# The delta rule's values turned token-major by block transposes and DRAM instead of products of the identity

## The chip, the core and the metric

The kernel runs on one core of a Trainium2 chip. The metric is device time in microseconds. The profile names TensorE's matmuls PE and its weight loads PEld, VectorE DVE, ScalarE ACT, GpSimd POOL; SPq is the queue of SyncE, from which nearly all DMAs are issued.

## The reference, cut to what matters

One encoder layer over 256 tokens of width 2048, in f32. The normalised input h feeds two token mixers, retention and a gated delta rule; their gated sum goes through an output projection; cross-attention, an MLP of width 8192 and a last norm follow. The change is in the delta rule, which has 16 heads of width 128:

```python
gqkv = jax.nn.silu(causal_conv(gqkv, conv_w)).astype(f32)
gq, gk, gv = jnp.split(gqkv, [GDN_HEADS * GDN_DK, 2 * GDN_HEADS * GDN_DK], axis=-1)
...
gv = gv.reshape(b, s, GDN_HEADS, GDN_DV)
...
u = t @ (vc * bc)            # values, token by token, into the chunk's triangular system
...
v_new = u_i - w_i @ state
```

The convolution and the SiLU act on every value channel along the tokens; the triangular system then needs the values with tokens on the rows.

## The kernel before

Weights are streamed once. `fetch` loads 1 MB into `raw` (three buffers, issued on SP), ScalarE rounds each half into `whi` (L108), VectorE takes the rest into `wlo` (L111), and TensorE multiplies both with the input held in SBUF. `blocks` gives 256 output channels as rows with the tokens along them (products L193 and L194); `chunk` gives tokens as rows (L151 to L153).

The delta rule's heads come in four groups of four, each group (`gdn_stream`) in two pairs of heads. For a pair, three calls of `blocks` give q, k and v channels. `evac` sends each head's 128 rows through `conv_silu`: ScalarE scales by the last tap, VectorE adds three shifted taps (L549), ScalarE applies the SiLU (L551). For v the result is the tile `vt`, 128 channels x 256 tokens, one for each head. The squares of q (L587, from the same two-slot tag as the accumulator) and the Gram products of k and q (L594 to L598) follow, then the decay factors (`alt`) and copies of small blocks of them (`cmp_l`, `pair32`, `pair64`). Near the end of the head's work TensorE transposes `vt` in two 128x128 products with the identity into a PSUM bank (L637), and ScalarE copies them to the head's part of `r4`, scaled by `nk`, the norm of k (L640). `r4` (one buffer, four heads) is read much later, by the triangular products of `gdn_core` (L722, L751), whose steps are dealt out between weight loads of the following stages; those of a group are finished before the next group takes `r4`.

Two round trips through DRAM are there already: `gdn_blocks` writes `cmp_l` to `scr_l` and reads it back as `lw`, and writes `tw` to `scr_t` and reads it back as `ct`; VectorE turns `ct` in 32x32 blocks into `cu` (L670).

The order of instructions on each engine, SP among them, is written by a planner that simulates the program in advance. Weight loads, their rounding and the evacuation of results have raised priority in it. At run time each engine and each queue goes through its list in order, and an instruction that waits holds up those behind it.

Of the kernel before, what the change touches and what calls it, by code (L numbers as in the profile page):

```python
# [10 lines left out]
F32 = mybir.dt.float32  # L11
F32R = mybir.dt.float32r
I32 = mybir.dt.int32
AF = mybir.ActivationFunctionType
# [3 lines left out]
P = 128  # L18
D = 2048
S = 256  # L20
NT = S // P
# [3 lines left out]
GH, GD = 16, 128  # L25
# [26 lines left out]
def trunk(ctx: ExitStack, tc: tile.TileContext, x, mem, positions, norm_mix_g, w_in, conv_w, gdn_a_log, gdn_dt_bias,  # L52
          ret_gn_g, gdn_norm_g, w_out, norm_x_g, norm_mem_g, w_xq, w_xkv, w_xo, norm_ffn_g, w_ff1, w_ff2,
          norm_final_g, inv_freq, out):
    nc = tc.nc
    PSUM = bass.MemoryType.PSUM
    act, vec, pool, pe = nc.scalar, nc.vector, nc.gpsimd, nc.tensor
# [7 lines left out]
    dram = ctx.enter_context(tc.tile_pool(name="scr", bufs=2, space=bass.MemoryType.DRAM))  # L65
# [6 lines left out]
    def bank():  # L72
        return psp.tile([P, 512], F32, name="b", tag="b", bufs=4)
# [10 lines left out]
    def finish_steps():  # L84
        while steps:
            step()
# [121 lines left out]
    ident = cp.tile([P, P], F32, name="ident")  # L208
# [129 lines left out]
    for k2 in range(8):  # L338
        ps = bank()
# [24 lines left out]
    for a in range(2):  # L364
        ps = bank()
# [166 lines left out]
    mx = mixer.enter_context(tc.tile_pool(name="mix", bufs=2))  # L532
# [8 lines left out]
    t64, u64, u128 = sparse("t64", 64), sparse("u64", 64), sparse("u128", NT, P)  # L541


    def conv_silu(blk, ps, dst):
        acc = mx.tile([P, S], F32, name="acc", tag="acc", bufs=2)
        act.activation(acc, ps, AF.Copy, scale=cw[:, 3, blk:blk + 1])  # L546
        for j in range(2, -1, -1):
            d = 3 - j
            vec.scalar_tensor_tensor(acc[:, d:], ps[:, :S - d], cw[:, j, blk:blk + 1], acc[:, d:],  # L549
                                     op0=ALU.mult, op1=ALU.add)  # L550
        act.activation(dst, acc, AF.Silu)  # L551

    def diag(alt):
        return alt.rearrange("p a n -> p (a n)")[:, 0:512].rearrange("p (t n) -> p t n", t=NT)[:, :, 0:P]

    def gdn_stream(grp):

        heads = []
        qe4 = mx.tile([P, 4, NT], F32, name="qe4", tag="qe4", bufs=2)
        for pr in range(2):  # L560
            h0 = grp * 4 + pr * 2
            dec = mx.tile([P, 2, 384], F32, name="dec", tag="dec", bufs=1)
            nc.sync.dma_start(dec, dec_d[h0:h0 + 2].rearrange("h p n -> p h n"))
            kq = mx.tile([P, 2, 2, S], F32, name="kq", tag="kq", bufs=1)
            vts = []
            for part, c0, bofs in ((1, C_GQ, 0), (0, C_GK, 16), (2, C_GV, 32)):
                def evac(b, ps, part=part, bofs=bofs):
                    if part < 2:
                        conv_silu(bofs + h0 + b, ps, kq[:, b, part, :])
                    else:  # L570
                        vt = mx.tile([P, S], F32, name="vt", tag="vt", bufs=2)
                        conv_silu(bofs + h0 + b, ps, vt)
                        vts.append(vt)
                blocks(h1, w_in[0], c0 + h0 * GD, 2, evac)
            if pr == 0:
                finish_steps()
                cmp_l = mx.tile([P, 8, 32], F32, name="cmp_l", tag="cmp", bufs=1)
                r4 = mx.tile([P, 4, NT, GD], F32, name="r4", tag="r4", bufs=1)
            grams = []
            ssk = mx.tile([P, 2, NT], F32, name="ssk", tag="ssk", bufs=2)  # L580
            for b in range(2):
                kh = mx.tile([P, 2, S], F32R, name="kh", tag="kh", bufs=2)
                kl = mx.tile([P, 2, S], F32R, name="kl", tag="kl", bufs=2)
                sq = mx.tile([P, S], F32, name="sq", tag="acc", bufs=2)
                act.activation(kh, kq[:, b], AF.Copy)
                vec.tensor_sub(kl, kq[:, b], kh.bitcast(F32))
                act.activation(sq, kq[:, b, 1], AF.Square)  # L587
                g0, g1 = bank(), bank()
                g0v = g0.rearrange("p (a n) -> p a n", a=2)
                g1v = g1[:, 0:256].rearrange("p (a n) -> p a n", a=2)  # L590
                if b == 0:
                    ssq = g1[:, 256:260].rearrange("p (b i) -> p b i", b=2)
                for t in range(NT):
                    pe.matmul(ssq[:, b, t:t + 1], sq[:, t * P:(t + 1) * P], ones[:, :1], start=True, stop=True)  # L594
                for n, (l, r) in enumerate(((kh, kh), (kh, kl), (kl, kh))):
                    pe.matmul(g0v, l[:, 0, 0:P], r, start=n == 0, stop=n == 2)  # L596
                for n, (l, r) in enumerate(((kh, kh), (kh, kl), (kl, kh))):
                    pe.matmul(g1v, l[:, 0, P:S], r[:, :, P:S], start=n == 0, stop=n == 2)  # L598
                grams.append((g0v, g1v))
                for t, src in enumerate((g0v[:, 0, 0:P], g1v[:, 0, :])):  # L600
                    dj = sm.tile([P, S], F32, name="dj", tag="bo", bufs=2)[:, :P]
                    vec.scalar_tensor_tensor(dj, src, 1.0, ident, op0=ALU.mult, op1=ALU.mult,
                                             accum_out=ssk[:, b, t:t + 1])
            ske = mx.tile([P, 2, NT], F32, name="ske", tag="ske", bufs=2)
            vec.tensor_scalar(ske, ssk, EPS, None, op0=ALU.add)
            vec.tensor_scalar(qe4[:, 2 * pr:2 * pr + 2, :], ssq, EPS * GD, EPS * EPS * GD,
                              op0=ALU.mult, op1=ALU.add)
            sc = mx.tile([P, 2, NT], F32, name="sc", tag="sc", bufs=2)
            vec.reciprocal(sc, ske)
            vec.tensor_mul(sc, sc, beta[:, :, h0:h0 + 2].rearrange("p t h -> p h t"))  # L610
            nk = mx.tile([P, 2, NT], F32, name="nk", tag="nk", bufs=2)
            pool.tensor_tensor(nk.rearrange("p b t -> p (b t)"), ske.rearrange("p b t -> p (b t)"), half_pow[:, :4], op=ALU.pow)
            for b in range(2):
                h, slot = h0 + b, pr * 2 + b
                g0v, g1v = grams[b]

                alt = mx.tile([P, 2, 384], F32, name="alt", tag="alt", bufs=4)
                vec.scalar_tensor_tensor(alt[:, :, 0:S], g0v, sc[:, b, 0:1],
                                         dec[:, b, 0:256].unsqueeze(1).to_broadcast([P, 2, 256]),
                                         op0=ALU.mult, op1=ALU.mult)  # L620
                vec.scalar_tensor_tensor(alt[:, :, S:384], g1v, sc[:, b, 1:2],
                                         dec[:, b, 256:384].unsqueeze(1).to_broadcast([P, 2, P]),
                                         op0=ALU.mult, op1=ALU.mult)
                for q in range(4):
                    ps_ = slice(32 * q, 32 * q + 32)
                    act.activation(cmp_l[ps_, 2 * slot:2 * slot + 2, :], diag(alt)[ps_, :, 32 * q:32 * q + 32], AF.Copy)

                for t in range(NT):
                    for a in range(2):
                        to, at = 64 * t + 32 * a, 64 * a  # L630
                        act.activation(pair32[to:to + 32, slot, to:to + 32],
                                       diag(alt)[at:at + 32, t, at + 32:at + 64], AF.Copy)
                    act.activation(pair64[64 * t:64 * t + 64, slot, 64 * t:64 * t + 64], diag(alt)[0:64, t, 64:P], AF.Copy)

                vps = bank()
                for t in range(NT):
                    pe.transpose(vps[:, t * P:(t + 1) * P], vts[b][:, t * P:(t + 1) * P], ident)  # L637
                r = r4[:, slot, :, :]
                for t in range(NT):
                    act.activation(r[:, t, :], vps[:, t * P:(t + 1) * P], AF.Copy, scale=nk[:, b, t:t + 1])  # L640
                heads.append(alt)
        return heads, cmp_l, r4, qe4

# [217 lines left out]
    for j in range(5):  # L861
        if j < 4:
            heads, cmp_l, r4, qe4 = gdn_stream(j)
# [80 lines left out]
    for h in range(XH):  # L944
# [17 lines left out]
        pr = xa.tile([P, NT, S], F32, name="pr", tag="pr", bufs=2)  # L962
# [36 lines left out]
    for c in range(4):  # L999
        for t in range(NT):  # L1000
            ps = bank()
# [95 lines left out]
```

## Time and profile before

| | |
|---|---|
| median of 3 runs | 2084.81 us (2084.80 to 2086.04) |
| the profiled execution, whole / its span | 2084.04 us / 2082.3 us |
| TensorE busy | 2066.1 us, 99% of the span |
| VectorE, ScalarE, GpSimd busy | 1402.3, 1120.3, 30.7 us |
| data moved by DMA | 405.90 MB in 314168 packets, 16288 of them under 512 B |
| granted clock of TensorE | 0.999 over the span |

Busy times are unions of an engine's instructions; matmuls are pipelined, their ends are modelled, and a second one begins before the first one's end. Lines such as L193 are those of the kernel before. In the timeline a row may merge several instructions (x3), and the bracket at its end says how long the engine was idle before it and what it waited for.

### The profile page before, as it was taken

How to read it: one execution, taken by the hardware profiler on the slowest of the kernel's cores; microseconds unless marked ns; L12 is line 12 of the kernel's file. 1: busy time of each engine (PE TensorE's matmuls, PEld its weight loads, DVE VectorE, ACT ScalarE, POOL GpSimd, SP SyncE). 2: the span in 40 equal slices, each digit the busy share in tenths (PEclk: the TensorE clock that was granted, in tenths of full speed). 3: DMA queues.
4: the chain of work that ended last, by engine and by line, in shares of the span. 5: the costliest groups of instructions: out<-in, count | busy, mean ns of one | idle time of the engine just before them, and what ended most of it. 6: DMA issues, size and time to landing. Idle time of an engine off the chain costs nothing.

```text
span 2082.3 us, 28611 instructions
## 1 busy us (share of the span) xinstructions
PE 2066.1 (99%) x11044; PEld 1783.3 (86%) x11044; DVE 1402.3 (67%) x2226; ACT 1120.3 (54%) x1844; POOL 30.7 (1%) x37
## 2 busy tenths in 40 slices
PE   8999999999999999999999999999999999999998
PEld 6888888888888888888888899888888888888887
DVE  5766879778757885778557665766556546645655
ACT  7674664675547555655446564654444434434444
POOL 0000000000000000000000000000000000000000
PEclk9999999999999999999999999999999999999999
DMA  8787666556555655565467664666566556656653
GB/s 299 246 274 248 199 192 195 166 179 194 188 162 190 193 179 164 188 187 189 152 214 239 193 189 146 187 198 193 191 194 191 193 191 192 192 195 189 194 191 141
DMA packets 314168, 405.90 MB, mean 195 GB/s; under 512 B 16288, under 2 KB 222128, under 8 KB 313904
## 3 DMA queue, kind: packets, MB, share of 16 engines
q1 hardware_dynamic: 313744, 403.55, 61.2%
q8 instruction: 86, 1.41, 0.3%
q10 hardware_dynamic: 288, 0.52, 0.1%
q14 instruction: 50, 0.41, 0.1%
HBM read 390.40 MB, written 13.65 MB: 194 GB/s over the span
## 4 chain that ended last, share of the span: by engine, by line
PE 97%; DMA 1%; ACT 1%; SPq 1%; DVE 0%; issue 0%; POOLq 0%; POOL 0%; ACTq 0%; DVEq 0%
PE s L193 33%; PE s L194 17%; PE s L152 14%; PE s L151 14%; PE s L153 14%; PE b L689 1%; PE b L596 1%; DMA xc<-x 1%; PE b L722 1%; PE b L122 0%; PE b L121 0%; PE b L123 0%; SPq L292 0%; ACT dec_w L501 0%; PE b L598 0%
## 5 line engine op out<-in xcount | busy, mean ns | idle before, releaser
L111 DVE TENSOR_TENSOR wlo<-raw,whi 128x1024 fp32r<-128x1024 f32 x702 | 857.8, 1223 | 515.1 <-ACT whi L108 508.5
L108 ACT ACTIVATE whi<-raw 128x1024 fp32r<-128x1024 f32 x702 | 742.7, 1059 | 688.7 <-PE s L153 341.7
L193 PE MATMUL s<-q,whi 128*128 128x512 f32 x3088 | 1062.4, 390 | 0.3 <-DVE q L986 0.3
L194 PE MATMUL s<-q,wlo 128*128 128x256 f32 x3088 | 845.0, 281 | 0.8 <-DVE wlo L111 0.8
L193 PEld LDWEIGHTS s<-q,whi 128*128 128x128 f32 x3088 | 570.7, 188 | 110.5 <-DVE q L986 0.5
L194 PEld LDWEIGHTS s<-q,wlo 128*128 128x128 f32 x3088 | 579.2, 188 | 14.3 <-DVE wlo L111 2.7
L152 PE MATMUL s<-wlo,q 128*128 128x512 f32 x1264 | 495.6, 392 | 0.7 <-DVE wlo L111 0.7
L153 PE MATMUL s<-whi,q 128*128 128x512 f32 x1264 | 492.2, 390 | 0.0
L151 PE MATMUL s<-whi,q 128*128 128x512 f32 x1264 | 451.5, 390 | 1.6 <-ACT q L255 1.6
L151 PEld LDWEIGHTS s<-whi,q 128*128 128x128 f32 x1264 | 237.3, 188 | 50.8 <-ACT q L255 2.0
L152 PEld LDWEIGHTS s<-wlo,q 128*128 128x128 f32 x1264 | 237.7, 188 | 48.9 <-DVE wlo L111 1.5
L153 PEld LDWEIGHTS s<-whi,q 128*128 128x128 f32 x1264 | 237.7, 188 | 47.7
L200 ACT ACTIVATE bo<-s 128x256 f32<-128x256 f32 x193 | 73.1, 379 | 119.2 <-PE s L194 106.0
L201 DVE TENSOR_TENSOR bo<-bo,s 128x256 f32<-128x256 f32 x193 | 80.4, 417 | 44.5 <-ACT bo L200 44.2
L549 DVE SCALAR_TENSOR_TENSOR acc<-bo,cw,acc 128x255 f32<-128x255 f32 (+1 forms) x144 | 66.8, 479 | 3.1 <-ACT acc L546 1.2
L658 DVE TENSOR_TENSOR pr<-lw,tw 32x31 f32<-32x31 f32 (+15 forms) x124 | 40.4, 326 | 10.7 <-DMA lw<-scr_l 8.6
L660 DVE TENSOR_TENSOR tw<-tw,pr 32x31 f32<-32x31 f32 (+15 forms) x124 | 40.6, 327 | 2.0
L1025 DVE SCALAR_TENSOR_TENSOR res<-s,rstd3q,res 128x512 f32<-128x512 f32 (+1 forms) x32 | 22.3, 735 | 12.0 <-PE s L153 12.0
L823 ACT ACTIVATE gth<-s 128x512 f32<-128x512 f32 x32 | 19.0, 592 | 20.7 <-PE s L153 15.1
L1014 DVE SCALAR_TENSOR_TENSOR hs<-bo 128x256 f32<-128x256 f32 x64 | 27.0, 421 | 1.1
L1017 DVE TENSOR_TENSOR q<-hs,q 128x256 fp32r<-128x256 f32 x64 | 26.8, 419 | 0.8 <-ACT q L1016 0.8
L1016 ACT ACTIVATE q<-hs 128x256 fp32r<-128x256 f32 x64 | 26.2, 410 | 0.0
(300 smaller groups left out, 1074.8 us busy)
## 6 DMA issues: line engine op xcount, KB each, us to landing
raw<-w_in SPq DMA_DIRECT2D x144, 1024.0 KB
raw<-w_ff SPq DMA_DIRECT2D x128, 1024.0 KB
raw<-w_xkv SPq DMA_DIRECT2D x31, 1024.0 KB
raw<-w_out SPq DMA_DIRECT2D x16, 1024.0 KB
raw<-w_xq SPq DMA_DIRECT2D x16, 1024.0 KB
raw<-w_xo SPq DMA_DIRECT2D x16, 1024.0 KB
dec_d<-dec_w SPq DMA_DIRECT2D x8, 384.0 KB
dec<-dec_d SPq DMA_DIRECT2D x8, 384.0 KB
```

The source lines that it names most:

```text
L108: rounding = act.activation(hi, src, AF.Copy)
L111: vec.tensor_sub(lo, src, hi.bitcast(F32))
L151: pe.matmul(o, xh, wh, start=first, stop=False)
L152: pe.matmul(o, xh, wl, start=False, stop=False)
L153: pe.matmul(o, xl, wh, start=False, stop=last)
L193: pe.matmul(ps[b], lh, xhl, start=kk == 0, stop=False)
L194: pe.matmul(ps[b][:, :S], ll, xh, start=False, stop=kk == KT - 1)
L200: act.activation(o, ps[b][:, S:], AF.Copy)
L201: vec.tensor_add(o, o, ps[b][:, :S])
L549: vec.scalar_tensor_tensor(acc[:, d:], ps[:, :S - d], cw[:, j, blk:blk + 1], acc[:, d:], op0=ALU.mult, op1=ALU.add)
L658: vec.tensor_mul(pv, lw[:, j, j + 1:32].unsqueeze(2).to_broadcast([32, n, j + 1]), tw[:, j, 0:j + 1].unsqueeze(1).to_broadcast([32, n, j + ...
L660: vec.tensor_sub(tw[:, j + 1:32, 0:j + 1], tw[:, j + 1:32, 0:j + 1], pv)
```

## The change

`conv_silu` gets a flag. With it (for v alone) the SiLU is written in place into the accumulator, and VectorE turns that, 128x256, in 32x32 blocks into the head's half of `vt`, which is now one tile for the pair, with one buffer. After the three `blocks` of a pair, four DMAs (one for each 32 partitions of `vt`) write the blocks to a DRAM tile `v_d` so that each token's 128 values stand in one row, in runs of 32 values (128 bytes); a fifth DMA reads `v_d` back into the pair's part of `r4`, tokens on the partitions. The two transposing products of each head and their PSUM bank go; the scaling by `nk` is done in place on `r4`.

```diff
-    def conv_silu(blk, ps, dst):
+    def conv_silu(blk, ps, dst, blocks_of=False):
...
-        act.activation(dst, acc, AF.Silu)
+        act.activation(acc if blocks_of else dst, acc, AF.Silu)
+        if blocks_of:
+            vec.transpose(dst, acc)
...
-            vts = []
+            vt = mx.tile([P, 2, S], F32, name="vt", tag="vt", bufs=1)
...
-                        vt = mx.tile([P, S], F32, name="vt", tag="vt", bufs=2)
-                        conv_silu(bofs + h0 + b, ps, vt)
-                        vts.append(vt)
+                        conv_silu(bofs + h0 + b, ps, vt[:, b], blocks_of=True)
...
+            v_d = dram.tile([2, S, GD], F32, name="v_d", tag="v_d", bufs=2)
+            for a in range(4):
+                nc.sync.dma_start(v_d[:, :, 32 * a:32 * a + 32].rearrange("h (b i) f -> i (h b) f", i=32),
+                                  vt[32 * a:32 * a + 32].rearrange("i h (b f) -> i (h b) f", f=32))
+            nc.sync.dma_start(r4[:, 2 * pr:2 * pr + 2], v_d.rearrange("h (t p) f -> p h t f", p=P))
...
-                vps = bank()
-                for t in range(NT):
-                    pe.transpose(vps[:, t * P:(t + 1) * P], vts[b][:, t * P:(t + 1) * P], ident)
                 r = r4[:, slot, :, :]
                 for t in range(NT):
-                    act.activation(r[:, t, :], vps[:, t * P:(t + 1) * P], AF.Copy, scale=nk[:, b, t:t + 1])
+                    act.activation(r[:, t, :], r[:, t, :], AF.Copy, scale=nk[:, b, t:t + 1])
```

## Rows read from the trace of the kernel before

**Rows 1.** The page, part 1: busy us, share of the span, instructions.

```profile
PE 2066.1 (99%) x11044; PEld 1783.3 (86%) x11044; DVE 1402.3 (67%) x2226; ACT 1120.3 (54%) x1844; POOL 30.7 (1%) x37
```

**Rows 2.** Busy us by stretch; then granted clock, DMA share, GB/s.

```profile
200.00:1293.00 1093.00, 1093.00 (x5955) 948.33 (x5954) 805.46 (x1424) 621.87 (x1089) 26.25 (x25) 1.00 0.59 186
```

**Rows 3.** Groups by line and form, L637: busy us, mean ns, idle before.

```profile
L637 PE MATMUL b<-ident,vt 128*128 128x128 f32 x32 | 6.1, 271 | 0.0
```

**Rows 4.** Timeline of TensorE's products: start us, us, instruction, count.

```profile
256.53 0.39 PE L193 MATMUL s<-q,whi 128*128 128x512 f32 x1
256.76 0.38 PE L637 MATMUL b<-ident,vt 128*128 128x128 f32 x2
...
257.09 0.39 PE L193 MATMUL s<-q,whi 128*128 128x512 f32 x1
...
257.44 0.38 PE L637 MATMUL b<-ident,vt 128*128 128x128 f32 x2
...
258.01 0.63 PE L193 MATMUL s<-q,whi 128*128 128x512 f32 x2
...
258.72 0.39 PE L193 MATMUL s<-q,whi 128*128 128x512 f32 x1
...
260.09 0.39 PE L193 MATMUL s<-q,whi 128*128 128x512 f32 x1
```

**Rows 5.** Instructions on the tile cu: ns min/median/max, first and last start.

```profile
L670 DVE STREAM_TRANSPOSE cu<-ct x4: 439/446/449, 371.3 to 973.8; 128x256 f32<-128x256 f32 x4
```

**Rows 6.** Groups by line and form on VectorE and ScalarE.

```profile
L111 DVE TENSOR_TENSOR wlo<-raw,whi 128x1024 fp32r<-128x1024 f32 x702 | 857.8, 1223 | 515.1 <-ACT whi L108 508.5
...
L200 ACT ACTIVATE bo<-s 128x256 f32<-128x256 f32 x193 | 73.1, 379 | 119.2 <-PE s L194 106.0 <-DVE dj L602 13.1
...
L640 ACT ACTIVATE r<-b,nk 128x128 f32<-128x128 f32 x32 | 9.6, 366 | 0.1
...
L551 ACT ACTIVATE vt<-acc 128x256 f32<-128x256 f32 x16 | 6.5, 406 | 0.3
```

**Rows 7.** Timeline of ScalarE, from 247 to 262 us.

```profile
247.29 0.40 ACT L551 ACTIVATE vt<-acc 128x256 f32<-128x256 f32 x1
247.72 0.42 ACT L587 ACTIVATE sq<-kq 128x256 f32<-128x256 f32 x1
251.40 0.38 ACT L200 ACTIVATE bo<-s 128x256 f32<-128x256 f32 x1 [3.26 <-DVE dj L602]
...
258.17 0.62 ACT L640 ACTIVATE r<-b,nk 128x128 f32<-128x128 f32 x2
```

**Rows 8.** Instructions on the tile ct: its reads as SP issues them.

```profile
L668 SPq DMA_DIRECT2D ct<-scr_t x16: 313/452/647, 363.8 to 967.5; - x16
```

**Rows 9.** Timeline of the SP queue, from 200 to 310 us.

```profile
216.68 32.35 SPq L98 DMA_DIRECT2D raw<-w_in  x7
256.72 0.37 SPq L563 DMA_DIRECT2D dec<-dec_d  x1
257.85 27.82 SPq L98 DMA_DIRECT2D raw<-w_in  x6
...
297.30 0.34 SPq L647 DMA_DIRECT2D scr_l<-cmp_l  x1
302.23 0.71 SPq L650 DMA_DIRECT2D lw<-scr_l  x2
303.03 0.41 SPq L98 DMA_DIRECT2D raw<-w_in  x1
```

**Rows 10.** Waits of the SP queue: total us, times, longest.

```profile
SPq L668 <- DMA scr_t<-tw: 9.4, 4, 3.7
...
SPq L650 <- DMA scr_l<-cmp_l: 7.5, 4, 4.6
```

**Rows 11.** Timeline of TensorE's products, from 405 to 409 us.

```profile
407.69 1.05 PE L722 MATMUL b<-r,u 128*128 128x128 f32 x8
```

**Rows 12.** Timeline of ScalarE, from 414 to 419 us.

```profile
417.75 0.40 ACT L551 ACTIVATE vt<-acc 128x256 f32<-128x256 f32 x1
```

## The prediction

> **What bounds the kernel now.** I read the busy times of the engines first, then the same by stretches, then the timelines of TensorE, ScalarE and the SP queue around one pair of heads. TensorE is busy 2066.1 of 2082.3 us [rows 1]; an average can hide idle stages, so the stretch counts: from 200 to 1293 us, in which all eight pairs of delta-rule heads lie, it is busy 1093.00 of 1093.00 us at a granted clock of 1.00 (the upper level, 2.4 GHz), while VectorE is busy 805.46, ScalarE 621.87 and the DMA engines 0.59 of the time [rows 2]. So in the stage that is changed only two things have a price: time that TensorE no longer spends, and lateness so large that TensorE runs dry. All else lies beside its products.
>
> **What goes.** 32 transposing products (two 128x128 halves for each of 16 heads). The group's row gives them 271 ns each and 6.1 us in union [rows 3]. Neither is what they cost, because consecutive products overlap. The timeline shows the price. The regular step of the input stream, from one first product (L193) to the next, is (260.09 - 258.72) / 4 = 0.34 us. With two transposes put in, a step takes 257.09 - 256.53 = 0.56, and the two steps that hold the next two take 258.01 - 257.09 = 0.92 [rows 4]. So two cost 0.22 to 0.24 us, about 0.11 each, the way back into the stream included, and there are 16 such couples, one for each head: 16 x 0.225 = 3.6 us. Since TensorE has no idle time here, all of that should come out of the end.
>
> One rule of the Trainium skill gives another price: "TensorE: Matmul & The Clock Gate", Part 4 (PE-mode transpose), has about 275 ns for a 128x128 transpose within a kernel. The row's 271 ns agrees with it as a duration, and by it the sum would be 8.8 us; the steps of rows 4 say that most of it overlaps.
>
> **What comes, engine by engine.**
> VectorE: 16 block transposes of 128x256 f32. The kernel has that very instruction elsewhere: 446 ns [rows 5], so 16 x 0.446 = 7.1 us on an engine with 287 idle us in the stretch [rows 2]. Cost at the end 0; without that cover 7.1.
>
> ScalarE: the SiLU writes in place, same size. The scaling by nk reads SBUF where it read PSUM, 366 ns each now [rows 6]; the nearest pair of forms, 128x256 from SBUF 406 and from PSUM 379 ns [rows 6], puts a half-width one at most 0.03 us dearer: 32 x 0.03 = 1 us on an engine 57% busy. 0.
>
> TensorE's next products: the Gram products' square sums need a tile of the same two-slot tag as the conv accumulator, which the transpose now frees instead of the SiLU. The squares came right behind the SiLU at 247.72 [rows 7]; they may now come up to one wlo subtraction (1.22 us [rows 6]) and one transpose (0.45) later, 1.7 us. Behind the waiting product TensorE's whole order would stand still: 0 if the planner puts stream products in between, 8 x 1.7 = 13 us if it never does. I take 0, because the planner knows engine times and its present order leaves TensorE no gap over 1093 us [rows 2], although these operations already hang together.
>
> SP: five more issues a pair, four writes of 32 partitions in 128-byte runs and one read. A comparable small issue takes 0.31 to 0.65, median 0.45 us [rows 8]: 40 x 0.45 = 18 us of a queue that mostly waits. Their data, 8 x 2 x 256 KB = 4.2 MB, are 1% of the 405.9 MB, in a stretch with 41% of DMA time free [rows 2]. No row shows 128-byte runs written to DRAM; I bound their landing below.
>
> **The new wait.** The scaling on ScalarE now waits for a chain: transpose, writes, read. Behind it on ScalarE stand the roundings of the weights (whi), for which TensorE waits. Behind the read on SP, which waits for the writes' landing, stand the weight loads. Worked for the first pair: the second head's SiLU ends at 247.69 [rows 7]; at most 1.7 us later it is transposed, 249.4; four issues, 251.2; the landing of the writes. The nearest is the scr_l write: issued from 297.30, and its readers leave at 302.23 [rows 9], the longest of four such waits being 4.6 us [rows 10]; the scr_t one is 3.7 at most. With 4.6: 255.8, and the same again for the read: 260.8 with its issue. The scalings used to stand at 258.17 [rows 7]. Left at that place, ScalarE would wait 2.6 us. It once stood still for 3.26 us (before 251.40 [rows 7]) without TensorE pausing. So 0; past that cover each further us costs 8 us in all, once a pair.
>
> For SP the same: seven weight loads before 249.03 keep a pace of (32.35 - 0.37) / 6 = 5.33 us, the last from 248.66. The next was due at 254.0 and left at 257.85, as SP waited until 256.72 with the load of dec [rows 9]. A read issued at 255.8 lies inside that wait and delays nothing. And how much lateness is free is seen behind the second pair: the last of six loads at 257.85 + 27.45 = 285.30, two paces of 27.45 / 5 = 5.5 later one is due at 296.3; it left at 303.03, 6.7 us late [rows 9], with TensorE still full [rows 2]. So 0 here as well.
>
> Reuse of buffers: r4 has one buffer, so the first read of a group waits for the last reader of the group before; that product runs at 407.69 [rows 11], the next group's second SiLU at 417.75 [rows 12], 10 us later. vt has one buffer now, refilled a pair (some 36 us) later. 0.
>
> **Sum.** 3.6 us off and 0 added. The profiled execution took 2084.04 us, 1.74 outside its span, which stays: 2080.4. The median of the runs is 0.77 above that execution, so 2081.2 us, 0.17% less. What a measurement of this kernel tells from no change is about 0.2%, 4.2 us: bounds 2080.6 and 2089.0.
>
> **Rivals.**
> *Slow writes (slower).* Place: SP's read, waiting for the four writes. If the writes land W after 251.2, the next weight load leaves at 252.0 + W (read and dec issued before it) against 254.0 due; 6.7 us late is free, so it decides from W = 8.7, and beyond 9.7 the kernel is slower by 0.2%. For it: twice the bytes of scr_l in 128-byte runs, and with 4.6 us for that, 9.2 for twice is near the edge; weight loads ahead in the same queue come on top. Against: the existing 128-byte reads (lw) sit in the same gaps harmlessly. At W = 11: 8 x 2.3 = 18 us, less 3.6: 2099.6. In "DMA: Bandwidth & Descriptors", Specifications, the Trainium skill wants 512 bytes or more for full rate and says that below it the engine reads, modifies and writes; no run here shows a write of that size.
>
> *Gain given back (no change).* The chain, or the squares behind the transposes, come later than the planner thinks by 0.45 us past the cover in each pair: 8 x 0.45 = 3.6, so 2084.8. For it: DMA waits are what the present order shows mis-timed [rows 10]. Against: those cost TensorE nothing.
>
> *Full durations.* If the transposes held TensorE for their whole 271 ns, 32 x 0.271 = 8.7 us would go: 2076.1. For it only rows 3; against it rows 4, where two of them lengthen the stream by 0.22 to 0.24.
>
> **How the numbers follow.** Forecast 0.64, by itself 2080.0 to 2082.6 (the price of a couple 0.22 to 0.24 us, and about 1 us for a new order); slow writes 0.18, gain given back 0.12, full durations 0.06. The range 2079.0 to 2090.0 holds the forecast, the second rival, and the mild quarter of the first (W up to 9.8). Faster by over 0.2%: the last rival and 0.3 of the forecast, 0.06 + 0.19 = 0.25. Slower: the first rival and a quarter of the second, 0.18 + 0.03 = 0.21. Within: 0.54.
>
> **What would show it.** No transposing products of vt; 16 block transposes near 446 ns; TensorE's busy time about 3.6 us less and still without idle time through the stage; SP's waits for the v_d writes below 8 us; ScalarE's wait for r below 3.3 us. It is wrong if TensorE shows idle time ended by whi, wlo or sq within the stage, or if its busy time falls by far more than 3.6 us.

## The result: 2092.7 us, slower, and the profile after

The changed kernel takes 2092.7 us (median of 6 runs, 2091.54 to 2094.49) against 2084.81: ratio 1.0037, 95% interval 1.0027 to 1.0047. The forecast was 2081.2 with a range to 2090.0; the time lies above the range, and the kernel became slower where it was to become faster.

The profiled execution took 2094.49 us. Part 1 of the page of the changed kernel, the row that answers to [rows 1]:

```profile
PE 2069.0 (99%) x11012; PEld 1780.2 (85%) x11012; DVE 1408.2 (67%) x2242; ACT 1119.6 (53%) x1844; POOL 29.9 (1%) x37
```

The 32 products are gone (11044 to 11012), but TensorE's busy time rose by 2.9 us. By stretches (busy us of PE, PEld, DVE, ACT, POOL, each with its number of instructions; then granted clock, DMA share, GB/s), the first row answers to [rows 2]:

```profile
200.00:1293.00 1093.00, 1085.49 (x5866) 937.05 (x5865) 806.45 (x1433) 617.29 (x1081) 25.46 (x25) 1.00 0.59 189
```

```profile
304.00:310.50 6.50, 4.96 (x15) 3.44 (x14) 5.28 (x9) 5.38 (x10) 0.00 (x0) 0.74 0.61 191
```

The stage that had no idle time has 7.5 us of it now. And behind one of the pauses the granted clock was 0.74 over 6.5 us, where it was 1.00 in the 8 us before: part of that stretch ran at the lower of the two levels (1.2 GHz), which is 6.5 x 0.26 = 1.7 us lost and part of the rise of the busy time. Two of the six executions have a mean clock of 0.998 and took 2094.4 and 2094.5; the other four have 0.999 and took 2091.5 to 2093.4. So the low clock comes with the loss in some executions and is not its bulk.

What TensorE waited for in the changed kernel (total us, times, longest):

```profile
PE s L152 <- DVE wlo L111: 3.8, 5, 2.1
PE s L194 <- DVE wlo L111: 2.9, 6, 0.5
...
PE s L151 <- ACT whi L108: 1.0, 1, 1.0
PE s L193 <- ACT whi L108: 1.0, 2, 0.6
```

Within the stage, all of it is weights that were rounded too late (`wlo` on VectorE follows `whi` on ScalarE). The transfers themselves came no later than forecast; ScalarE's timeline and SP's show why the rounding was late. First ScalarE in the first pair, the stretch that answers to [rows 7]:

```profile
248.07 0.40 ACT L551 ACTIVATE acc<-acc 128x256 f32<-128x256 f32 x1
...
249.86 1.06 ACT L108 ACTIVATE whi<-raw 128x1024 fp32r<-128x1024 f32 x1 [1.08 <-PE s L193]
250.82 0.40 ACT L593 ACTIVATE sq<-kq 128x256 f32<-128x256 f32 x1
254.79 0.38 ACT L200 ACTIVATE bo<-s 128x256 f32<-128x256 f32 x1 [3.57 <-DVE dj L608]
255.15 1.06 ACT L108 ACTIVATE whi<-raw 128x1024 fp32r<-128x1024 f32 x1
...
258.87 1.28 ACT L643 ACTIVATE r<-r,nk 128x128 f32<-128x128 f32 x4 [1.37 <-DMA r<-v_d]
...
260.68 1.04 ACT L108 ACTIVATE whi<-raw 128x1024 fp32r<-128x1024 f32 x1
261.63 1.04 ACT L632 ACTIVATE cmp_l<-alt 32x64 f32<-32x64 f32 x4
...
263.97 1.05 ACT L632 ACTIVATE cmp_l<-alt 32x64 f32<-32x64 f32 x4
...
265.80 1.06 ACT L108 ACTIVATE whi<-raw 128x1024 fp32r<-128x1024 f32 x1
```

The second squares run at 250.82; they were at 247.72 [rows 7], 0.78 us of which is lateness from before the stage. ScalarE then stops 3.57 us for `dj` (the diagonal sums, which use the same buffers as `bo`), rounds three weight halves from 255.15 to the one at 265.80 where TensorE uses one every 2.75 us (8 steps of 0.34), stands 1.37 us for the read of `v_d`, and after the scaling the small copies (`cmp_l`, `pair`) fill it. The half at 265.80 is the one TensorE pauses for at 266.6. The kernel before rounded the same three halves, counted from the start, at 254.87, 260.99 and 262.56; small copies ran ahead of its scaling (at 258.17 [rows 7]), and behind its stop ScalarE waited for nothing until 264:

```profile
254.87 1.06 ACT L108 ACTIVATE whi<-raw 128x1024 fp32r<-128x1024 f32 x1
255.84 1.03 ACT L626 ACTIVATE cmp_l<-alt 32x64 f32<-32x64 f32 x4
...
258.68 1.04 ACT L626 ACTIVATE cmp_l<-alt 32x64 f32<-32x64 f32 x4
...
260.99 1.06 ACT L108 ACTIVATE whi<-raw 128x1024 fp32r<-128x1024 f32 x1
...
262.56 1.05 ACT L108 ACTIVATE whi<-raw 128x1024 fp32r<-128x1024 f32 x1
```

The SP queue of the same pair, beside [rows 9]:

```profile
249.91 3.34 SPq L582 DMA_DIRECT2D v_d<-vt  x4
256.24 0.38 SPq L584 DMA_DIRECT2D r<-v_d  x1
258.53 0.39 SPq L98 DMA_DIRECT2D raw<-w_in  x1
```

The writes are issued by 253.25 and have landed at 256.24, 3.0 us later; the next weight load leaves at 258.53, where it left at 257.85 before, which is no later once the 0.78 us are taken off. The waits of all engines and then of SP in the changed kernel:

```profile
ACT bo L200 <- DVE dj L608: 14.4, 4, 3.6
...
DVE pr L661 <- DMA lw<-scr_l: 13.6, 4, 5.7
...
ACT r L643 <- DMA r<-v_d: 8.3, 7, 2.0
```

```profile
SPq L584 <- DMA v_d<-vt: 24.6, 15, 3.4
```

The last row has seven waits for the read: 1.4 to 2.0 us in four pairs (both of the first group, the first of the third and fourth), 0.6 at most in three; the first pair of the second group has none. The first row names `dj` four times; the other four pairs have a stop of 3.4 to 3.7 us there too (`bo` for TensorE in one, the copies `pair` for VectorE's `alt` in three).

A second loss is in the middle row: VectorE stands up to 5.7 us for `lw`, the read-back of the small blocks. The chain of waits of the changed kernel there (start us, us, what):

```profile
479.97 0.37 SPq L98
...
480.39 0.40 SPq L653
...
481.69 7.35 DMA lw<-scr_l
...
489.16 0.19 DVE pr L661
...
490.54 1.22 DVE wlo L111
```

A weight load of 1 MB left at 479.97, 0.4 us ahead of the four reads of `lw`; the last of them took 7.35 us to land, `wlo` stands behind them on VectorE, and TensorE pauses 2.1 us. Before, a load left 1.35 us ahead of the same reads (467.46 and 468.81), with a stop of 1.7 us. That the load makes the difference is not shown: in the first group before, a load stands between the reads themselves [rows 9], and VectorE's stop there is 2.7 us, the longest of the four in the kernel before:

```profile
DVE pr L658 <- DMA lw<-scr_l: 8.6, 4, 2.7
```

Where the time went can be read off the products themselves. Their order in the weight stream is the same in all kernels, so the n-th product L193 or L151 of a kernel is set against the n-th of the kernel before; the table has the median difference of their starts, in us, around that time of the kernel before (e1 to e13 are the experiments below; the figure at 195 is start-up, ahead of the change). Each row is one execution, the profiled one; e2's took 4.1 us more than the median of its runs.

```
             195    278    330    413    450    500    633    670    730    850    885   1270
after       0.78   1.51   4.85   4.85   5.51   7.46   7.50   8.94   9.64   9.63  10.71  10.28
e2          1.32   3.61   7.06   8.02   8.73  10.64  10.68  12.20  12.73  12.71  14.04  13.60
e4          0.64   0.53   1.48   2.57   2.22   2.55   2.59   2.48   2.80   2.79   2.58   5.26
e10         0.66   1.14   2.60   2.60   2.31   2.77   2.81   3.27   4.34   4.32   5.39   4.96
e7          1.24   1.12   1.32   1.32   0.94   1.16   1.20   1.10   0.67   0.66   0.46   0.05
e13         1.01   0.95   1.52   1.52   2.18   1.68   1.69   1.60   1.37   1.37   1.85   1.64
e1          0.88   0.43   0.46   1.32   1.00   0.56  -0.12  -0.76  -1.02  -1.00  -1.46  -1.79
```

In the row "after" the loss comes in seven steps: behind the first pair of every group (278, 450, 670, 885), behind the second pair of the first group (330: 3.3 us, with the low clock), and at the `lw` reads (500, 730). The five pairs make 7.3 us of it, the `lw` reads 2.7. One of the five, the first pair of the second group (0.7 us), has no wait for the read; there the scaling, behind all small copies, stands just ahead of a rounding.

### The profile page after: what moved, and what is told of

The parts are those of the page before. It is cut to its first block, busy times and chain, and to the rows that moved or that the text cites. A ratio compares the mean times of both kernels' runs of the same rounds, so it can differ in the third digit from the quotient of the medians.

```text
span 2092.8 us, 28623 instructions
## 1 busy us (share of the span) xinstructions
PE 2069.0 (99%) x11012; PEld 1780.2 (85%) x11012; DVE 1408.2 (67%) x2242; ACT 1119.6 (53%) x1844; POOL 29.9 (1%) x37
## 4 chain that ended last, share of the span: by engine, by line
PE 89%; DMA 4%; ACT 3%; SPq 1%; DVE 1%; issue 1%; POOLq 0%; POOL 0%; ACTq 0%; DVEq 0%
PE s L193 31%; PE s L194 16%; PE s L152 12%; PE s L153 12%; PE s L151 12%; DMA v_d<-vt 1%; ACT whi L108 1%; DVE wlo L111 1%; DMA r<-v_d 1%; DMA lw<-scr_l 1%; PE b L692 1%; DMA xc<-x 1%; PE b L725 1%; SPq L582 1%; PE b L122 0%
## 5 line engine op out<-in xcount | busy, mean ns | idle before, releaser
L193 PE MATMUL s<-q,whi 128*128 128x512 f32 x3088 | 1063.4, 391 | 1.3 <-ACT whi L108 1.0
L193 PEld LDWEIGHTS s<-q,whi 128*128 128x128 f32 x3088 | 570.6, 188 | 114.2 <-ACT whi L108 2.6
L151 PE MATMUL s<-whi,q 128*128 128x512 f32 x1264 | 451.9, 391 | 3.0 <-ACT q L255 2.0
L151 PEld LDWEIGHTS s<-whi,q 128*128 128x128 f32 x1264 | 237.4, 188 | 52.6 <-ACT q L255 2.4
L661 DVE TENSOR_TENSOR pr<-lw,tw 32x31 f32<-32x31 f32 (+15 forms) x124 | 40.4, 326 | 15.6 <-DMA lw<-scr_l 13.6
```

Source lines behind the costliest of these rows:

```text
L151: pe.matmul(o, xh, wh, start=first, stop=False)
L193: pe.matmul(ps[b], lh, xhl, start=kk == 0, stop=False)
L661: vec.tensor_mul(pv, lw[:, j, j + 1:32].unsqueeze(2).to_broadcast([32, n, j + 1]), tw[:, j, 0:j + 1].unsqueeze(1).to_broadcast([32, n, j + ...
```

## The experiments

Every run stands beside runs of the kernel before on the same chip; these vary more than at first (medians 2085.39, 2086.09, 2085.39, 2085.41), so the ratio counts. In the expectations the theories are: W, ScalarE waits for the read; S, SP holds weight loads back; Q, the squares wait for the block transpose; L, VectorE's stops for `lw`; C, the stop for `dj` has spent the cover.

**e1: what the products cost.** The kernel before without them.

```diff
-                vps = bank()
-                for t in range(NT):
-                    pe.transpose(vps[:, t * P:(t + 1) * P], vts[b][:, t * P:(t + 1) * P], ident)
...
-                    act.activation(r[:, t, :], vps[:, t * P:(t + 1) * P], AF.Copy, scale=nk[:, b, t:t + 1])
+                    act.activation(r[:, t, :], vts[b][:, t * P:(t + 1) * P], AF.Copy, scale=nk[:, b, t:t + 1])
```

> The kernel before without the 32 transposing products: the scaling reads vt as it stands, so the values are not turned token-major (left out on purpose, to price the products). Nothing else is added. If a product costs its step of 0.11 us: 2084.8 - 3.6 = 2081.2 us. If it costs its whole 271 ns: 2076.1. If the planner's new order costs as much as the products: 2084.8.

Measured 2083.3, ratio 0.9991 (0.9982 to 1.0000): 1.9 us less, at most 3.8. The forecast of 3.6 is at the edge of the interval, the full durations (8.7) are outside it. The table has 2.7 us from 195 to 1270.

**e2: the scaling written later.**

```diff
-                r = r4[:, slot, :, :]
-                for t in range(NT):
-                    act.activation(r[:, t, :], r[:, t, :], AF.Copy, scale=nk[:, b, t:t + 1])
...
     # at the head of gdn_core
+        for i in range(4):
+            for t in range(NT):
+                act.activation(r4[:, i, t, :], r4[:, i, t, :], AF.Copy, scale=nks[i // 2][:, i % 2, t:t + 1])
```

> The changed kernel with the scaling of r4 by the norm of k moved out of the pair's work into the first step of gdn_core, many us after the read has landed. Theory W (ScalarE stands waiting for the read of v_d just where it has no time left, and the roundings of the weights behind it come late): 2081 to 2085. Theory S (SP's wait for the written v_d holds back weight loads): about 2091, as after. Theory Q (the squares of q wait for a transpose, so the Gram products and all small copies behind them come some 3 us later into a full ScalarE): 2088 to 2092.

Measured 2093.92, ratio 1.0043 (1.0030 to 1.0055): no gain. That speaks neither for nor against W, for the edit did not move the work. ScalarE's timeline of this kernel:

```profile
260.96 1.28 ACT L695 ACTIVATE r<-r,nk 128x128 f32<-128x128 f32 x4 [1.65 <-DMA r<-v_d]
```

The planner drew the scaling forward to the same place, with much the same wait.

**e3: the squares in other buffers.**

```diff
-                sq = mx.tile([P, S], F32, name="sq", tag="acc", bufs=2)
+                sq = mx.tile([P, S], F32, name="sq", tag="rb", bufs=2)
```

> The changed kernel with the squares of q in the buffers of another tag (rb), so that they don't wait for the accumulator that the block transpose still reads. Theory Q: most of the loss goes, 2082 to 2086. Theory W: 2089 to 2092, the wait for the read is untouched. Theory S: 2091.

Measured 2083.98, ratio 0.9991 (0.9982 to 1.0000): the loss is gone, as Q has it, but more moved than was meant. Its waits (all engines) have no stop of `bo` for `dj` any more, since without the shared buffers the Gram products went far forward; the stops for `lw` stayed, and three waits for the read.

```profile
DVE pr L661 <- DMA lw<-scr_l: 14.4, 4, 5.7
...
ACT r L643 <- DMA r<-v_d: 4.1, 3, 2.4
```

**e4: everything done, but nobody waits for the read.**

```diff
-            nc.sync.dma_start(r4[:, 2 * pr:2 * pr + 2], v_d.rearrange("h (t p) f -> p h t f", p=P))
+            rj = mx.tile([P, 512], F32, name="rj", tag="g_sq", bufs=1).rearrange("p (h t f) -> p h t f", h=2, t=NT)
+            nc.sync.dma_start(rj, v_d.rearrange("h (t p) f -> p h t f", p=P))
...
-                    act.activation(r[:, t, :], r[:, t, :], AF.Copy, scale=nk[:, b, t:t + 1])
+                    act.activation(r[:, t, :], vt[:, b, t * P:(t + 1) * P], AF.Copy, scale=nk[:, b, t:t + 1])
```

> The changed kernel with all its transposes and transfers, but the read of v_d goes into an idle tile and the scaling reads the block-transposed vt (the values are not turned token-major, left out on purpose). ScalarE then waits for no transfer, while VectorE, SP and the DMA engines do all the work of the change. Theory W: 2081 to 2085. Theory S: 2091, since SP waits as before. Theory Q: 2088 to 2092.

Measured 2090.29, ratio 1.0022 (1.0013 to 1.0032). The median looks like Q's or S's, the trace doesn't: the steps behind the first pairs are gone (table), and what is lost is one pause of 2.8 us at 923 us, smaller ones at the `lw` reads, whose stops grew, and one of 0.7 us for `ct` at 373:

```profile
DVE pr L662 <- DMA lw<-scr_l: 18.0, 4, 6.4
...
PE s L152 <- DVE wlo L111: 4.9, 7, 2.8
```

ScalarE's timeline of the first pair has the late squares (250.69) and the stop of the changed kernel, and the scaling without a wait, ahead of the small copies:

```profile
254.66 0.39 ACT L200 ACTIVATE bo<-s 128x256 f32<-128x256 f32 x1 [3.57 <-DVE dj L609]
...
256.65 1.26 ACT L644 ACTIVATE r<-vt,nk 128x128 f32<-128x128 f32 x4
...
259.07 1.04 ACT L108 ACTIVATE whi<-raw 128x1024 fp32r<-128x1024 f32 x1
```

So without W the pairs' pauses go, though stop and shift stay, and a second loss, L, stands beside it. A run's time alone would have misled here.

**e5: the late squares alone.** The kernel before, with its products.

```diff
         act.activation(dst, acc, AF.Silu)
+        if blk >= 32:
+            vec.transpose(acc, acc)
```

> The kernel before, transposing products and all, with one thing added: VectorE turns the v accumulator in place after the SiLU has read it (its result is read by nothing), so that the accumulator's buffer, and with it the squares of q, wait for VectorE as in the changed kernel. No transfers. Theory Q alone (the late squares are enough): 2088 to 2094. Theory Q and W together (late squares only cost where ScalarE must wait for the read as well): 2084 to 2086.

Measured 2086.38 against 2086.09, ratio 1.0001 (0.9992 to 1.0009); TensorE is busy for all but 0.2 us of the stretch:

```profile
200.00:1293.00 1093.00, 1092.80 (x5943) 946.36 (x5942) 809.06 (x1439) 621.22 (x1089) 25.62 (x25) 1.00 0.59 186
```

The squares come as late as in the changed kernel (250.51 for the second, against 250.82), and the stop for `dj` is as long (3.57 us). So the late squares with that stop, and VectorE's 16 turns, cost nothing by themselves that this interval (0.1%, 2 us) would show.

**e6: the transfers on another queue.**

```diff
-                nc.sync.dma_start(v_d[:, :, 32 * a:32 * a + 32].rearrange("h (b i) f -> i (h b) f", i=32),
+                nc.gpsimd.dma_start(v_d[:, :, 32 * a:32 * a + 32].rearrange("h (b i) f -> i (h b) f", i=32),
...
-            nc.sync.dma_start(r4[:, 2 * pr:2 * pr + 2], v_d.rearrange("h (t p) f -> p h t f", p=P))
+            nc.gpsimd.dma_start(r4[:, 2 * pr:2 * pr + 2], v_d.rearrange("h (t p) f -> p h t f", p=P))
```

> The changed kernel with the five transfers of a pair issued on GpSimd's queue in place of SP's. Squares and the wait for the read stay. Theory L (SP, held up by the landing of v_d, lets a weight load go just ahead of the small reads lw, VectorE stands still for 5.7 us for them, and TensorE pauses at 489 and 712 us): those pauses go, about 3 us less, 2088 to 2090. If SP's part costs nothing: 2091 to 2094. If the transfers take longer on this queue, ScalarE's wait for the read grows: over 2094.

Measured 2086.06 against 2086.09, ratio 0.9998 (0.9989 to 1.0007): better than any of the three expected. GpSimd's issues take longer (medians 0.65 and 0.81 us for a write and the read, 0.55 and 0.38 on SP), and the planner put the scaling later, at 262.3 for the first pair instead of 258.9; ScalarE's waits for the read fall from 8.3 us in 7 to 2.6 us in 4. A pause of 1.0 us for `lw` stays. So this run does not price SP's part; it took most of W away too.

**e7: the scaling really moved.** The lines that it takes out are those of e2.

```diff
     # in gdn_core, last: ScalarE's second copy into pair32
+        with tc.issue_after(last):
+            for i in range(4):
+                for t in range(NT):
+                    act.activation(r4[:, i, t, :], r4[:, i, t, :], AF.Copy, scale=nks[i // 2][:, i % 2, t:t + 1])
```

> As e2, but the scaling is tied behind ScalarE's first copy in gdn_core, so that it can't be drawn forward to the pair's own work as it was there. The squares still wait for the block transpose. Theory Q alone: 2089 to 2093. Theory Q and W together: the pauses in the pairs go (at 267, 304, 439, 666 and 886 us) and those for lw stay, 2083 to 2087.

Measured 2083.52, ratio 0.9988 (0.9979 to 0.9996): all that the change lost is back, with late squares, the stop for `dj` and all transfers on SP as they were (SP's longest wait for the writes is 3.3 us). S is out. Its stretch and its stops:

```profile
200.00:1293.00 1093.00, 1092.62 (x5929) 945.92 (x5929) 811.24 (x1441) 621.78 (x1089) 23.99 (x25) 1.00 0.61 190
```

```profile
ACT bo L200 <- DVE dj L608: 14.4, 4, 3.6
...
DVE pr L659 <- DMA lw<-scr_l: 9.4, 4, 4.0
```

**e8: e3 and e6 together.** Both diffs above.

> The changed kernel with both cures: the squares in another tag (e3) and the transfers on GpSimd's queue (e6). Theory L with Q: all pauses of TensorE in the stage go and only the products' saving is left, 2081 to 2082.5, under the kernel before and under e3 (2084.0). If lw's waits have another cause: 2083.5 to 2085. If the longer way of the transfers brings ScalarE's wait back: over 2086.

Measured 2086.83 against 2086.09, ratio 1.0004 (0.9995 to 1.0013): a miss for L with Q, and the time of the third case. ScalarE waits up to 2.7 us for the read again, as that case has it, but the two pauses of TensorE, 1.7 us at 307 and 0.8 us at 481, stand behind VectorE's stops for `lw` (up to 4.7 us). Two cures don't add, since each is also a new order.

**e9: the changed kernel again.** No edit.

> The changed kernel unchanged, as the measure for the two that follow on the same chip: 2091 to 2095, ratio to the kernel before 1.003 to 1.005, with the same places of pause (267, 304, 439, 489, 666, 712, 886 us).

Measured 2095.02, ratio 1.0049 (1.0036 to 1.0061), with pauses at 267, 305, 441, 491, 667, 714 and 887 us.

**e10: without the stop for `dj`.**

```diff
-                    dj = sm.tile([P, S], F32, name="dj", tag="bo", bufs=2)[:, :P]
+                    dj = sm.tile([P, 512], F32, name="dj", tag="junk", bufs=1)[:, :P]
```

> The changed kernel with the tile dj (the diagonal sums, L607) out of the tag that the evacuation bo uses, so that ScalarE no longer stands still for 3.6 us before each pair's first evacuation; the squares' wait and the wait for the read stay. Theory C (ScalarE's cover for a weight half is one and is spent by the stop for dj, so that the wait for the read a few us later is no longer covered): the pauses of the pairs go and those for lw stay, 2083 to 2087. If the stop for dj has no part in it: 2090 to 2094.

Measured 2089.22, ratio 1.0019 (1.0010 to 1.0029): 6 us less than e9, between the two expectations. The stop for `dj` is gone by name, but in the first pair three shorter waits stand in its place:

```profile
249.51 0.39 ACT L200 ACTIVATE bo<-s 128x256 f32<-128x256 f32 x1 [0.85 <-PE s L194]
...
252.49 0.51 ACT L546 ACTIVATE acc<-bo,cw 128x256 f32<-128x256 f32 x1 [1.07 <-PE b L600]
...
254.82 0.42 ACT L551 ACTIVATE kq<-acc 128x256 f32<-128x256 f32 x1 [1.82 <-DVE acc L549]
```

They come to 3.7 us, and ScalarE's waits for the read (9.6 us in all, 3.3 at the longest) even grew. The steps in the table come to 4.3 us against 9.5, but not where the stop was: the low clock went (1.7 us), the `lw` step at 500 fell by 1.5, the one at 450, whose pair stops for TensorE in both kernels, by 0.9, the one at 670 by 1.0; those at 278 (0.5) and 885 (1.1) hardly changed. So this run does not take ScalarE's idle time away, and theory C, that the stop spends the cover, is neither shown nor refuted by it.

**e11: `lw` on another queue.** e3, and:

```diff
-        nc.sync.dma_start(scr_l, cmp_l.rearrange("p g n -> p (g n)"))
+        nc.gpsimd.dma_start(scr_l, cmp_l.rearrange("p g n -> p (g n)"))
...
-            nc.sync.dma_start(lw[8 * q:8 * q + 8], scr_l[32 * q:32 * q + 32, :].rearrange("m (g n) -> g m n", g=8))
+            nc.gpsimd.dma_start(lw[8 * q:8 * q + 8], scr_l[32 * q:32 * q + 32, :].rearrange("m (g n) -> g m n", g=8))
```

> e3 (squares in another tag) with the round trip of cmp_l (scr_l and lw) issued on GpSimd's queue, so that it no longer stands behind weight loads in SP's queue. Theory L (VectorE's 5.7 us stops for lw are the pauses left in e3 at 479 and 699 us, 2.8 us): those pauses go, 2081 to 2082.5, against 2084.0 for e3. If the data come late for another reason: 2083.5 to 2086.

Measured 2085.41 against 2085.39, ratio 1.0003 (0.9994 to 1.0011): a miss. The pauses at the `lw` reads did shrink (0.4 us at the longest, 4.3 us the longest stop), yet the time is no lower than e3's 2083.98. Where the rest went is not settled: the trace has 1.8 us of pauses in the stage against 3.5 in e3, while the medians say the reverse. Part of that is the choice of execution: e3's profiled one took 2085.93, e11's 2085.22.

**e12: e3 and e7 together.**

> e3 and e7 together: squares in another tag and the scaling tied into gdn_core. All transfers on SP. Theory Q and W: nothing of the pairs' pauses is left; with the pauses for lw as small as in e7 2081 to 2083, the fastest of all and 0.1 to 0.2% under the kernel before; with those of e3 2083 to 2085.

Measured 2083.32 against 2085.39, ratio 0.9989 (0.9980 to 0.9998). With e7 the fastest; the two can't be told apart.

**e13: the squares' wait alone.** As e3, but each square tied behind the SiLU of its head, where it was before.

```diff
-                sq = mx.tile([P, S], F32, name="sq", tag="acc", bufs=2)
+                sq = mx.tile([P, S], F32, name="sq", tag="rb", bufs=2)
...
-                act.activation(sq, kq[:, b, 1], AF.Square)
+                with tc.issue_after(silus[b]):
+                    act.activation(sq, kq[:, b, 1], AF.Square)
```

> The changed kernel with the squares in another tag as in e3, but each tied behind the SiLU of its value head on ScalarE, where the kernel before had it. e3 let the planner draw the Gram products far forward and took the stop for dj away with them; here both stay, and only the wait of the squares for the block transpose goes. If ScalarE's wait for the read and the stop for dj are enough by themselves (W with C): 2089 to 2094, pauses near 267, 304, 440, 666 and 886 us. If the late squares are needed as well (Q): 2082 to 2086, none of those pauses.

Measured 2086.56 against 2085.41, ratio 1.0005 (0.9996 to 1.0014). ScalarE's timeline of this kernel:

```profile
248.61 0.40 ACT L596 ACTIVATE sq<-kq 128x256 f32<-128x256 f32 x1
252.41 0.38 ACT L200 ACTIVATE bo<-s 128x256 f32<-128x256 f32 x1 [3.40 <-PE s L194]
...
255.90 1.07 ACT L108 ACTIVATE whi<-raw 128x1024 fp32r<-128x1024 f32 x1
256.87 1.03 ACT L635 ACTIVATE cmp_l<-alt 32x64 f32<-32x64 f32 x4
...
259.48 1.28 ACT L646 ACTIVATE r<-r,nk 128x128 f32<-128x128 f32 x4 [0.29 <-DMA r<-v_d]
...
262.47 1.06 ACT L108 ACTIVATE whi<-raw 128x1024 fp32r<-128x1024 f32 x1
```

The stop of 3.4 us ahead of the evacuation is nearly as long as ever, though it now ends with a product and not with `dj`. But with the squares 2.2 us earlier, the small copies are ready while the read is under way: four `cmp_l` copies run ahead of the scaling, ScalarE waits 0.29 us in place of 1.37 (0.85 at most in any pair), and the steps in the table are 0.7 us or less. So the loss of the four pairs that wait needs both: the wait for the read (without it, e4, e5 and e7, the late squares are free there) and the late squares (without them most of the wait is filled with work). The step of the fifth pair, at 450, is 0.7 us here too; it is not the wait's, and is gone where the scaling runs earlier (e4) or elsewhere (e7).

## Why the prediction was wrong

**The bound was right.** TensorE, without idle time, sets the end in this stage; every loss found is a pause of it or, once, its low clock.

**What goes** was nearly right. The saving forecast at 3.6 us measured 1.9 (0 to 3.8) in e1, and the durations' 8.7 lies far outside that.

**VectorE and the transfers were right.** The block transpose takes 438 ns a time where 446 was taken, and e5 shows that 16 of them cost nothing within its 0.1%. The scaling from SBUF takes 391 ns, not 366 (0.03 dearer, as bounded). The groups of the changed kernel that answer to [rows 5, 6]:

```profile
L643 ACT ACTIVATE r<-r,nk 128x128 f32<-128x128 f32 x32 | 10.2, 391 | 8.3 <-DMA r<-v_d 8.3
...
L553 DVE STREAM_TRANSPOSE vt<-acc 128x256 f32<-128x256 f32 x16 | 7.0, 438 | 0.0
```

**The rival "slow writes" fell in its mechanism**, though its sign came true. It decided from a landing 8.7 us after the last issue; the writes landed 3.0 us after it in the first pair, and SP's longest wait for them is 3.4. (The four issues took 3.3 us where 1.8 were taken; the landing, taken as 4.6, made up for it.) So the 128-byte runs never became a price at the end here; against them spoke the rule that the prediction cites from the Trainium skill ("DMA: Bandwidth & Descriptors", Specifications). With SP's waits left as they were, e7 is faster than the kernel before.

**The step that failed** is "The new wait", with the one on the squares before it: each was set to 0 by itself. The sizes were about right. ScalarE's wait for the read was put at 2.6 us at most; it is 1.4 to 2.0 in the four pairs that pause for it. The squares were put at most 1.7 us later; net of the lateness ahead of the stage they came 2.3 later, with a rounding of 1.06 us now ahead of the second one. But the cover was counted twice. The 3.26 us stop before 251.40 [rows 7] was read as "ScalarE can stand still for 3.26 us for nothing". A stop of that size did not happen once: it is in every pair, a few us ahead of the scaling, and the new wait comes on top of it; the late squares shift the copies that would have filled the new wait to behind it. What the runs show in place of "0 past that cover": in the first pair, right behind the stop, wait and shifted copies lie in one stretch of 11 us in which TensorE needs four weight halves and gets three. Over the 17 us behind the second head's SiLU, ScalarE is idle for 3.7 us before and 6.2 in the changed kernel; it is 4.9 in e4, 5.1 in e5 and e7, and 4.1 in e13. e5 and e7 (stop and shift without wait) and e13 (stop without shift, little wait) are each within 0.15% of the kernel before, and e4 (stop and shift without wait) has no pause at the pairs; all together cost 0.37 to 0.49%, of which the `lw` reads are about a quarter. That the stop is needed for the loss is argued from this account; no run takes it away alone (e10 splits it, e3 moves the squares too).

**SP's lateness** was set to 0 because a load 6.7 us late had done no harm. That holds for the weight loads. What was not asked is what a shifted load does to the small reads behind it: VectorE's stops for `lw` rose from 8.6 us in all (2.7 at the longest) to 13.6 (5.7), and the steps at 500 and 730 are 2.0 and 0.7 us. These stops are seen in the traces of the changed kernel, e3 and e4; that a shifted load makes them is argued, and that e11 shortened them without getting the time back leaves their exact price open.

**The second rival, gain given back,** named the right places and the wrong price: 0.45 us a pair, where the first pairs of the groups lost 0.7 to 1.4 us net of the saving, and the second pair of the first group 3.3 with the low clock.

## What to carry to other kernels

An idle stretch that cost nothing does not show how much cover is left for the next one: lay all stops of one engine that fall between two deliveries to the bounding engine on one line, old and new, and add the work that shifts into the gap. When a step is moved to another engine, ask whose buffer it now holds: here a value's accumulator, shared by tag with the squares, shifted work that had nothing to do with the change. And where a planner writes the order, an edit may be undone (e2) or bring another order with it (e3, e6, e8), so the place of the moved instruction is to be looked up in the timeline before a time is read as a verdict.

The round trip can be used: with the scaling tied into `gdn_core` (e7) the kernel takes 0.9988 (0.9979 to 0.9996) of the time before, and so with e12. Leaving the turning out altogether gives no less within the noise (e1, 0.9991).

## What the runs showed of the hardware

In the profiled execution of the changed kernel, pauses of TensorE of 1.0 and 0.5 us between 304 and 306.5 us were followed by a granted clock of 0.74 over the 6.5 us; e10, whose pauses there were 0.8 and 0.5 us, shows 1.00 over the same 6.5 us. (In e9 and e2, where the same pauses were 1.2 and 1.1 us and again 0.5, it was 0.76 and 0.74 over as long a stretch.) The length of a single pause does not tell: 2.1 us at 490 us in that execution, 1.7 us in e8 and 2.8 us in e4 were followed by no fall of the clock. One of four reads of `lw` (128 KB in all) landed 7.35 us after its issue, behind a weight load of 1 MB that left 1.7 us earlier in the same queue. The 256 KB of a pair, written in runs of 128 bytes, landed 3.0 us after the last issue.
